# A hybrid layer on one core: the states' single steps split into three parts, VectorE ahead of ScalarE on the scan's bank, the gate's tail on GpSimd and ScalarE

## The chip, the core and the metric

The kernel runs on one core of one Trainium2 chip. A core has a matrix engine (TensorE, PE in the profile; its weight loads are PEld), a vector engine (VectorE, DVE), an activation engine (ScalarE, ACT), a general engine (GpSimd, POOL) and a queue engine that issues DMAs (SyncE, SP). Each engine works through its own queue in order; semaphores tie the queues together. The metric is the time of one execution on the device in microseconds, the median of the runs.

## The reference

One layer of a hybrid decoder is computed for a prompt of 1024 tokens and, with the same weights, for one new token of each of 8 running sequences (1032 columns in all), in 32-bit floats. After a norm, one input projection feeds two mixers: a gated linear recurrence of 8 heads (HGRN2) and a Mamba-2 mixer of 16 heads in two groups. Their outputs go through one output projection, and a gated MLP with a short convolution follows. What matters here is the Mamba-2 mixer:

```python
xbc = silu(causal_dwconv(xbc_r, buf_s, conv_w, conv_b))      # 12 tiles of 128 channels
xs, Bm, Cm = split(xbc)                                      # x: 16 heads of 64; B, C: 2 groups of 128
dt = softplus(dt_r + dt_bias);  A = -exp(a_log)
y, S = ssd_scan(xs * dt, A * dt, Bm, Cm, S0)                 # chunks of 128 tokens
y = y + d * xs
y = rmsnorm(y * silu(z)) * ssm_norm_w                        # the gate, per group of 512 channels
```

For the 8 running sequences the scan has length one: `S = exp(A*dt) * S0 + (xs*dt) outer B` and `y = S . C + d * xs`. All states S are outputs.

## The kernel before

The activations lie transposed, 128 channels on the partitions and the 1032 columns along the free dimension. A 32-bit product is made of three matmuls on split operands (high by high, low by high, high by low). The input projection is a list of jobs, one for each tile of 128 output channels; `in_job` runs one as three chunks of 344 columns with 24 matmuls each, so 72 a job, and after each chunk an `evict` takes the result out of its PSUM bank. The Mamba jobs are x8, x10 (B and C of group 0, made first), x0 to x3 (x of group 0), then x9, x11 (B and C of group 1) and x4 to x7 (x of group 1). After them come z0 to z3 (the gate of group 0), the four jobs of head 0 (f, q, v, sg), z4 to z7 and the rest of the heads. `xbc_evict` and `xbc_close` do the convolution: a copy on ACT, small copies on DVE (L346, L348), one scaling on ACT (L332), three multiply-adds on DVE (L334) and the silu on ACT (L356).

The work between the projections' matmuls comes in streams. `ssd(g)` is the scan of group g: for each of 8 chunks of 128 tokens a front (`ssd_front`) and a back (`ssd_back`). The front loads two blocks csb of cumulated decays, makes exponentials of them on ACT (L530, L531), puts a transpose of B and the product of B and C side by side into one bank `bg`, takes the first out with an ACT copy (L537) and the second, times a triangular mask, with DVE (L538), both into one tile `bt`, transposes x into the bank `xp`, and makes xdt (DVE, L543), xde (POOL, L544) and csb times the masked product (DVE, L546). The back makes the outputs and the next state (yo, st, yd on PE; L563, L569, L579, L582 on DVE; L568 on POOL).

`decode_bc(g)` transposes B and C of the 8 single tokens and writes them to a DRAM scratch bc_d, from which `ssm_decode(g, i)` reads them back, spread over all partitions. `ssm_decode` is the single step of one tile of group g. For each of two halves of the batch it issues three loads (Bb and Cb from bc_d, the state Sd), scales the state on ACT (L627, four instructions), makes Bb times x (DVE, L628), adds it to the state (DVE, L629), stores the state, multiplies it by Cb on POOL (L631) and sums that on DVE (L632). A last small DVE instruction (L633) puts the result back into the tile. All of this is emitted in one go.

The gate's jobs `z` evict through a silu on ACT (L659), multiply on DVE (L660), square on ACT and add up in gacc on POOL or DVE (L665). 36 matmuls (50 for group 1) after a chunk of the fourth, `rstd` makes the norm's factor (L637 to L640), and after the last chunk `tail` multiplies the four tiles of the group by the norm's weight and by gacc, on DVE (L683), and stores them to mix_d. Head 0's levels follow on group 1's tail: `scale` makes products on DVE (L853, L854) and copies on ACT (L856, L857), which PE's matmuls `a` read.

The order on PE is the order in which the program is written: `drive` emits the matmuls of a stream among those of the jobs by a weight, and `after(n, work)` puts work in after n more matmul steps. The other engines' instructions are ordered by a planner which knows dependencies and estimated times; each engine's queue is in order. Loads made through `fetch` are held behind the last weight load.

Of the kernel before, what the change touches and what calls it, by code (L numbers as in the profile page):

```python
# [16 lines left out]
P = 128  # L17
# [33 lines left out]
def hybrid_layer(  # L51
# [19 lines left out]
    def nm(s):  # L71
        cnt[0] += 1
        return f"{s}_{cnt[0]}"
# [18 lines left out]
    def mm(out, lhsT, rhs, start=True, stop=True):  # L92
        PE.matmul(out, lhsT, rhs, start=start, stop=stop)  # L93
# [256 lines left out]
    def xbc_close(j, ext):  # L350
# [6 lines left out]
        A.activation(acc[:, T:NT], acc[:, T + 3:T + 32:4], AF.Silu)  # L357
        return acc

    def xbc_job(j, put):  # L360
        ext = []
        def begin():
            ext.append(xbc_open())
            if j in (5, 7):
                ssm_decode(0, (5, 7).index(j))

        in_job(f"x{j}", OFF_X + j * P, lambda c, cs, ps: xbc_evict(j, ext[0], c, cs, ps), begin=begin, end=lambda: put(xbc_close(j, ext[0])))

# [150 lines left out]
    def ssd_front(g, c, parts):  # L519
        tsl = slice(c * P, (c + 1) * P)  # L520
        hc = c * 16 + g * 8
        lm = []
        for q in range(2):
            csb = half("csb")
            csb3 = csb.rearrange("p (h l) -> p h l", l=P)
            h0 = hc + q * 4
            fetch(csb, cs_d[0, h0:h0 + 4, :].rearrange("h l -> (h l)").unsqueeze(0).to_broadcast([P, 512]))

            for h in range(4):
                A.activation(csb3[:, h, :], csb3[:, h, :], AF.Relu, scale=-1.0, bias=cst[:, h0 + h:h0 + h + 1])  # L530
            A.activation(csb, csb, AF.Exp, scale=-1.0)  # L531
            lm.append(csb3)
        bg = bank("bg")
        PE.transpose(bg[:, 0:P], BT[g][:, tsl], ident)
        mm(bg[:, P:2 * P], BT[g][:, tsl], CT[g][:, tsl])
        bt = small.tile([P, 2, P], F32, tag="bt", bufs=2, name=nm("bt"))
        A.copy(bt[:, 0, :], bg[:, 0:P])  # L537
        V.tensor_tensor(bt[:, 1, :], bg[:, P:2 * P], tri, op=ALU.mult)  # L538
        xp = bank("xp")
        for i in range(4):  # L540
            PE.transpose(xp[:, i * P:(i + 1) * P], Xg[g][i][:, tsl], ident)
        xdt, xde = half("xdt"), half("xde")
        V.tensor_tensor(h64(xdt), h64(xp), b64(dt, hc), op=ALU.mult)  # L543
        G.tensor_tensor(h64(xde), h64(xdt), b64(dec, hc), op=ALU.mult)  # L544
        for csb3 in lm:
            V.tensor_tensor(csb3, csb3, bt[:, 1:2, :].to_broadcast([P, 4, P]), op=ALU.mult)  # L546
        parts[c] = g, c, bt, xdt, xde, lm

    def ssd_back(parts, at_c):
        g, c, bt, xdt, xde, lm = parts.pop(at_c)  # L550
        tsl = slice(c * P, (c + 1) * P)
        hc = c * 16 + g * 8
        Xc = [Xg[g][i][:, tsl] for i in range(4)]
        if c:
            ecs = half("ecs")
            ecs3 = ecs.rearrange("p (j l) -> p j l", l=P)
            for h2 in range(2):
                fetch(ecs3[h2 * 64:(h2 + 1) * 64],
                      cs_d[1, hc:hc + 8, :].rearrange("(j h) l -> h j l", h=2)[h2:h2 + 1].to_broadcast([64, 4, P]))
            yo = bank("yo")  # L560
            for i in range(4):
                mm(yo[:, i * P:(i + 1) * P], S[g][:, i * P:(i + 1) * P], CT[g][:, tsl])
            V.tensor_tensor(ecs, yo, ecs, op=ALU.mult)  # L563
        st = bank("st")
        mm(st, bt[:, 0, :], xde)
        Sn = half("S")
        if c:
            G.tensor_tensor(h64(Sn), h64(S[g]), b64(etot, hc), op=ALU.mult)  # L568
            V.tensor_tensor(Sn, Sn, st, op=ALU.add)  # L569
        else:  # L570
            V.tensor_copy(Sn, st)
        S[g] = Sn
        yd = bank("yd")
        for hh in range(8):
            mm(yd[(hh % 2) * 64:(hh % 2) * 64 + 64, (hh // 2) * P:(hh // 2 + 1) * P],
               xdt[:, hh * 64:(hh + 1) * 64], lm[hh // 4][:, hh % 4, :])
        ya = yd.rearrange("p (j l) -> p j l", l=P)
        if c:
            V.tensor_tensor(ecs, yd, ecs, op=ALU.add)  # L579
            ya = ecs3  # L580
        for i in range(4):
            V.scalar_tensor_tensor(Xc[i], Xc[i], d_bc[:, g * 4 + i:g * 4 + i + 1], ya[:, i, :],  # L582
                                   op0=ALU.mult, op1=ALU.add)
# [16 lines left out]
    def d4(t):  # L600
        return t.rearrange("p (b n) -> p b n", n=P)
# [10 lines left out]
        SP.dma_start(bc_d[2 * g:2 * g + 2].rearrange("i b n -> b i n"), bcr.rearrange("b (i n) -> b i n", n=P))  # L612

    def ssm_decode(g, i):
        j = g * 4 + i
        xdd = small.tile([P, 2, ND], F32, tag="xdd", name=nm("xdd"))
        xdec = Xg[g][i][:, T:NT]
        V.tensor_tensor(xdd[:, 0, :], xdec, ddb[:, 0, j, :], op=ALU.mult)
        for b0 in (0, 4):
            bs = slice(b0, b0 + 4)  # L620
            Bb, Cb = tl("d", "Bb")[:, :512], tl("d", "Cb")[:, :512]
            for t_, r in ((Bb, 2 * g), (Cb, 2 * g + 1)):
                fetch(t_, bc_d[r, bs].rearrange("b n -> (b n)").unsqueeze(0).to_broadcast([P, 512]))
            Sd = tl("ld", "Sd")
            fetch(d4(Sd), state_ssm[0, bs, 2 * j:2 * j + 2].rearrange("b h p n -> (h p) b n"))
            for b in range(4):
                A.activation(d4(Sd)[:, b, :], d4(Sd)[:, b, :], AF.Copy, scale=ddb[:, 1, j, b0 + b:b0 + b + 1])  # L627
            V.tensor_tensor(d4(Bb), d4(Bb), cb(xdd[:, 0, bs]), op=ALU.mult)  # L628
            V.tensor_tensor(Sd, Sd, Bb, op=ALU.add)  # L629
            SP.dma_start(ssm_sample[0, bs, 2 * j:2 * j + 2].rearrange("b h p n -> (h p) b n"), d4(Sd))  # L630
            G.tensor_tensor(Cb, Sd, Cb, op=ALU.mult)  # L631
            V.tensor_reduce(xdd[:, 1, bs], d4(Cb), axis=mybir.AxisListType.X, op=ALU.add)  # L632
        V.scalar_tensor_tensor(xdec, xdec, d_bc[:, j:j + 1], xdd[:, 1, :], op0=ALU.mult, op1=ALU.add)  # L633

    def rstd_of(dst, tmp, ps, n):

# [5 lines left out]
    def ssm_gate(g):  # L642
        acc = []

        def z_job(i):
            j = g * 4 + i

            def begin():
                if i == 0:
                    acc.append(tl("g", "gacc"))  # L650
                if g:
                    ssm_decode(1, i)
                elif i < 2:
                    ssm_decode(0, i + 2)

            def evict(c, cs, ps):
                Y = Xg[g][i][:, cs]
                sz = tl("z", "sz")[:, :CH]
                A.activation(sz, ps, AF.Silu)  # L659
                V.tensor_tensor(Y, Y, sz, op=ALU.mult)  # L660
                if i == 0:
                    A.activation(acc[0][:, cs], Y, AF.Square)
                else:
                    A.activation(sz, Y, AF.Square)
                    (V if g or i == 3 else G).tensor_tensor(acc[0][:, cs], acc[0][:, cs], sz, op=ALU.add)  # L665
                if i == 3:
                    after(36 + 14 * g, lambda: rstd(c))
            in_job(f"z{j}", OFF_Z + j * P, evict, begin=begin)

        def rstd(c):  # L670
            cs = chunks[c]
            ps = bank("ms", "nx")
            mm(ps[:, :CH], ones, acc[0][:, cs])
            rstd_of(acc[0][:, cs], tl("z", "nt")[:, :CH], ps[:, :CH], 512)

            if c == NCH - 1:
                tail()

        def tail():
            for i in range(4):  # L680
                j = g * 4 + i
                Y = Xg[g][i][:, :NT]
                V.scalar_tensor_tensor(Y, Y, col("sn", j), acc[0][:, :NT], op0=ALU.mult, op1=ALU.mult)  # L683
                SP.dma_start(mix_d[8 + j], Y)

        for i in range(4):
            z_job(i)
# [13 lines left out]

    def ssd(g):
        parts = {}
        decode_bc(g)
        yield 6.5
        ssd_front(g, 0, parts)
        for c in range(1, NC):
            yield 2.5
            ssd_front(g, c, parts)
            yield 2.5  # L710
            ssd_back(parts, c - 1)
        yield 3.0
        ssd_back(parts, NC - 1)
        yield 1.0
        ssm_state_out(g)
# [366 lines left out]
                out_job(r0, m, (hf,), r0 == 4)  # L1082

    with tc.manual_schedule(engines={mybir.EngineType.PE}):
        finish("x3")
        drive(ssd(0), 45.5, "x7")
        drive(ssd(1), 45.5, "v0")
        finish("z7")
        for h in range(H):
            drive(head(h, heads[h]), 32.0 if h else 35.0, f"sg{h + 1}" if h < H - 1 else "o12.2")  # L1090
        finish("o12.6")
        for r0 in (0, 4):
            mixes[r0] = mix_load(r0)
# [363 lines left out]
```

## Time and profile before

| | us |
|---|---|
| median of 3 runs | 1786.03 (1785.04 to 1788.24) |
| profiled execution's own time | 1782.61 |
| its span | 1780.9 |
| PE busy | 1725.4 |
| DVE busy | 1119.3 |
| ACT busy | 817.5 |
| POOL busy | 405.3 |

The profiled execution is 3.4 us below the median of the runs shown. The instructions that the change touches lie between about 97 us (job x3) and 420 us (the first levels of head 0): the scan of group 0 from 116 us, its gate's tail at 294 us, the scan of group 1 from about 225 us and its gate's tail at 403 us. In the windows the first column is the stretch, then its length, the busy time of PE, PEld, DVE, ACT and POOL with their instructions, PE's granted clock as a share of full speed, the DMA engines' busy share and GB/s. A line of waits reads: the waiting engine, tile and line, the one it waited for, the sum in us, how often, and the longest. A timeline line reads: start, length, engine, line, operation, out<-in, shapes, and in brackets the idle time just before and what ended it. In groups by tile the three durations are the least, median and greatest in ns, then the first and last start.

### The profile page before, as it was taken

What the parts mean: (1) busy time and instruction counts of PE and PEld (TensorE: products, weight loads), DVE (VectorE), ACT (ScalarE), POOL (GpSimd) and SP (SyncE); (2) the same over time, 40 slices, a digit from 0 to 9 for tenths busy, and PEclk for the clock granted to TensorE, in tenths of its full rate; (3) what the DMA queues carried; (4) which work ended last, traced back from release to release, by engine and by line L of the source; (5) the groups of instructions that cost most, each with busy time, mean ns of one, the idle gap of its engine ahead of it and who ended that gap; (6) DMA issues with size and microseconds to landing.
All of it is one profiled execution on the core that took longest, in us unless ns stands there. A gap on an engine that the chain in (4) does not pass through costs nothing. (4 is left out here: it accounts for less than half of the span.)

```text
span 1780.9 us, 38506 instructions
## 1 busy us (share of the span) xinstructions
PE 1725.4 (97%) x16143; PEld 1675.6 (94%) x16143; DVE 1119.3 (63%) x2011; ACT 817.5 (46%) x1464; POOL 405.3 (23%) x415
## 2 busy tenths in 40 slices
PE   7999899999999999999999978999999999999998
PEld 6998799999999999999899978999999999999997
DVE  6667966575564565458645768666666666445545
ACT  7677688455554454545333435334333344111114
POOL 2113331220110111011000364554445542000001
PEclk9999999999999999999999998999999999999999
DMA  4144634642221222234334432222222225422212
GB/s 154 39 126 126 189 106 132 184 137 98 87 66 51 86 73 78 58 109 155 101 108 133 135 90 72 72 72 78 82 91 72 72 84 203 152 81 90 97 61 96
DMA packets 218019, 182.34 MB, mean 102 GB/s; under 512 B 13388, under 2 KB 195158, under 8 KB 217830
## 3 DMA queue, kind: packets, MB, share of 16 engines
q1 hardware_dynamic: 217558, 179.80, 32.3%
q8 instruction: 126, 2.06, 0.5%
q14 instruction: 47, 0.39, 0.1%
q0 software_dynamic: 288, 0.10, 0.0%
HBM read 141.53 MB, written 38.52 MB: 101 GB/s over the span
## 5 line engine op out<-in xcount | busy, mean ns | idle before, releaser
L93 PE MATMUL mm<-hh,wh 128*128 128x344 f32 x1248 | 405.3, 325 | 0.3 <-issue 0.2
L93 PE MATMUL mm<-hl,wh 128*128 128x344 f32 x1248 | 404.5, 324 | 0.0
L93 PE MATMUL mm<-hh,wl 128*128 128x344 f32 x1248 | 402.0, 322 | 0.0
L93 PEld LDWEIGHTS mm<-hh,wh 128*128 128x128 f32 x1248 | 235.0, 189 | 3.9 <-issue 2.6
L93 PEld LDWEIGHTS mm<-hl,wh 128*128 128x128 f32 x1248 | 235.2, 189 | 2.4 <-issue 0.9
L93 PEld LDWEIGHTS mm<-hh,wl 128*128 128x128 f32 x1248 | 235.3, 189 | 2.2 <-issue 1.5
L183 ACT CAST wh<-ws 128x1024 fp32r<-128x1024 f32 x96 | 100.5, 1047 | 242.8 <-PE dn L93 135.3
L93 PE MATMUL ub<-ul,wh 128*128 128x258 f32 x704 | 200.4, 285 | 4.3 <-DVE ul L1144 4.3
L93 PE MATMUL ub<-uh,wh 128*128 128x258 f32 x704 | 200.3, 285 | 2.0 <-ACT uh L1143 2.0
L93 PE MATMUL ub<-uh,wl 128*128 128x258 f32 x704 | 200.2, 284 | 0.0
L93 PE MATMUL dn<-ah,wh 128*128 128x256 f32 (+1 forms) x640 | 181.1, 283 | 1.2 <-DVE x L1387 1.2
L93 PE MATMUL dn<-al,wh 128*128 128x256 f32 (+1 forms) x640 | 180.6, 282 | 0.0
L93 PE MATMUL dn<-ah,wl 128*128 128x256 f32 (+1 forms) x640 | 180.2, 282 | 0.0
L184 DVE TENSOR_TENSOR wl<-ws,wh 128x1024 fp32r<-128x1024 f32 x96 | 126.4, 1317 | 72.4 <-ACT wh L183 71.4
L93 PE MATMUL mm<-mh,wh 128*128 128x258 f32 x512 | 147.7, 288 | 11.2 <-DVE x L1040 8.3
L93 PE MATMUL ua<-ul,wh 128*128 128x258 f32 x528 | 149.4, 283 | 0.9 <-DVE ul L1144 0.9
L93 PE MATMUL ua<-uh,wh 128*128 128x258 f32 x528 | 149.2, 283 | 0.0
L93 PE MATMUL ua<-uh,wl 128*128 128x258 f32 x528 | 148.4, 281 | 0.0
L93 PE MATMUL mm<-ml,wh 128*128 128x258 f32 x512 | 145.8, 285 | 0.7 <-DVE ml L999 0.7
L93 PE MATMUL mm<-mh,wl 128*128 128x258 f32 x512 | 145.9, 285 | 0.0
L93 PEld LDWEIGHTS ub<-ul,wh 128*128 128x128 f32 x704 | 134.5, 191 | 5.0 <-DVE ul L1144 5.0
L93 PEld LDWEIGHTS ub<-uh,wh 128*128 128x128 f32 x704 | 134.0, 190 | 2.5 <-ACT uh L1143 2.5
(347 smaller groups left out, 3942.8 us busy)
## 6 DMA issues: line engine op xcount, KB each, us to landing
ws<-in_w_in_dram SPq DMA_DIRECT2D x52, 512.0 KB
ws<-in_w_up_dram SPq DMA_DIRECT2D x44, 512.0 KB
ws<-in_w_out_dram SPq DMA_DIRECT2D x24, 512.0 KB
act_d<-val SPq DMA_DIRECT2D x22, 516.0 KB
al<-act_d SPq DMA_DIRECT2D x22, 516.0 KB
ws<-in_w_down_dram SPq DMA_DIRECT2D x22, 512.0 KB
ml<-mix_d SPq DMA_DIRECT2D x48, 172.0 KB
csb<-cs_d SPq DMA_DIRECT2D x32, 256.0 KB
```

What stands on the lines that cost most here:

```text
L93: PE.matmul(out, lhsT, rhs, start=start, stop=stop)
L183: A.copy(wh[:, :n], ws[:, :n])
L184: V.tensor_tensor(wl[:, :n], ws[:, :n], wh[:, :n].bitcast(F32), op=ALU.subtract)
```

## The change

- `ssm_decode` is cut into three: the loads when it is called, the states (scaling, product, sum, store, POOL product) 30 matmul steps later, the outputs (the two sums over Cb and the last small instruction) 30 steps after that. The small xdd product moves from the call to the states.
- The single steps of group 0 begin with the jobs x3, x11, x5 and x7 in place of x5, x7, z0 and z1. Those of group 1 stay at z4 to z7.
- `decode_bc(0)` is emitted after job x2, ahead of x3, in place of after x3.
- In `ssd_front` the tile bt is parted into bt and bc; DVE's masked product out of the bank bg is written ahead of ACT's copy out of the same bank.
- In the gate's tail the DVE instruction on 128x1032 is replaced by a POOL multiply by gacc and an ACT scaling by the norm's weight, in place, four of each per group.

```diff
--- before.py
+++ after.py
@@ -357,12 +357,15 @@
         A.activation(acc[:, T:NT], acc[:, T + 3:T + 32:4], AF.Silu)
         return acc
 
+
+    DEC0 = (3, 11, 5, 7)
+
     def xbc_job(j, put):
         ext = []
         def begin():
             ext.append(xbc_open())
-            if j in (5, 7):
-                ssm_decode(0, (5, 7).index(j))
+            if j in DEC0:
+                ssm_decode(0, DEC0.index(j))
 
         in_job(f"x{j}", OFF_X + j * P, lambda c, cs, ps: xbc_evict(j, ext[0], c, cs, ps), begin=begin, end=lambda: put(xbc_close(j, ext[0])))
 
@@ -533,9 +536,9 @@
         bg = bank("bg")
         PE.transpose(bg[:, 0:P], BT[g][:, tsl], ident)
         mm(bg[:, P:2 * P], BT[g][:, tsl], CT[g][:, tsl])
-        bt = small.tile([P, 2, P], F32, tag="bt", bufs=2, name=nm("bt"))
-        A.copy(bt[:, 0, :], bg[:, 0:P])
-        V.tensor_tensor(bt[:, 1, :], bg[:, P:2 * P], tri, op=ALU.mult)
+        bt, bc = (small.tile([P, P], F32, tag=s_, bufs=2, name=nm(s_)) for s_ in ("bt", "bc"))
+        V.tensor_tensor(bc, bg[:, P:2 * P], tri, op=ALU.mult)
+        A.copy(bt, bg[:, 0:P])
         xp = bank("xp")
         for i in range(4):
             PE.transpose(xp[:, i * P:(i + 1) * P], Xg[g][i][:, tsl], ident)
@@ -543,7 +546,7 @@
         V.tensor_tensor(h64(xdt), h64(xp), b64(dt, hc), op=ALU.mult)
         G.tensor_tensor(h64(xde), h64(xdt), b64(dec, hc), op=ALU.mult)
         for csb3 in lm:
-            V.tensor_tensor(csb3, csb3, bt[:, 1:2, :].to_broadcast([P, 4, P]), op=ALU.mult)
+            V.tensor_tensor(csb3, csb3, bc.unsqueeze(1).to_broadcast([P, 4, P]), op=ALU.mult)
         parts[c] = g, c, bt, xdt, xde, lm
 
     def ssd_back(parts, at_c):
@@ -562,7 +565,7 @@
                 mm(yo[:, i * P:(i + 1) * P], S[g][:, i * P:(i + 1) * P], CT[g][:, tsl])
             V.tensor_tensor(ecs, yo, ecs, op=ALU.mult)
         st = bank("st")
-        mm(st, bt[:, 0, :], xde)
+        mm(st, bt, xde)
         Sn = half("S")
         if c:
             G.tensor_tensor(h64(Sn), h64(S[g]), b64(etot, hc), op=ALU.mult)
@@ -612,10 +615,11 @@
         SP.dma_start(bc_d[2 * g:2 * g + 2].rearrange("i b n -> b i n"), bcr.rearrange("b (i n) -> b i n", n=P))
 
     def ssm_decode(g, i):
+
         j = g * 4 + i
         xdd = small.tile([P, 2, ND], F32, tag="xdd", name=nm("xdd"))
         xdec = Xg[g][i][:, T:NT]
-        V.tensor_tensor(xdd[:, 0, :], xdec, ddb[:, 0, j, :], op=ALU.mult)
+        ts_ = []
         for b0 in (0, 4):
             bs = slice(b0, b0 + 4)
             Bb, Cb = tl("d", "Bb")[:, :512], tl("d", "Cb")[:, :512]
@@ -623,14 +627,26 @@
                 fetch(t_, bc_d[r, bs].rearrange("b n -> (b n)").unsqueeze(0).to_broadcast([P, 512]))
             Sd = tl("ld", "Sd")
             fetch(d4(Sd), state_ssm[0, bs, 2 * j:2 * j + 2].rearrange("b h p n -> (h p) b n"))
-            for b in range(4):
-                A.activation(d4(Sd)[:, b, :], d4(Sd)[:, b, :], AF.Copy, scale=ddb[:, 1, j, b0 + b:b0 + b + 1])
-            V.tensor_tensor(d4(Bb), d4(Bb), cb(xdd[:, 0, bs]), op=ALU.mult)
-            V.tensor_tensor(Sd, Sd, Bb, op=ALU.add)
-            SP.dma_start(ssm_sample[0, bs, 2 * j:2 * j + 2].rearrange("b h p n -> (h p) b n"), d4(Sd))
-            G.tensor_tensor(Cb, Sd, Cb, op=ALU.mult)
-            V.tensor_reduce(xdd[:, 1, bs], d4(Cb), axis=mybir.AxisListType.X, op=ALU.add)
-        V.scalar_tensor_tensor(xdec, xdec, d_bc[:, j:j + 1], xdd[:, 1, :], op0=ALU.mult, op1=ALU.add)
+            ts_.append((bs, Bb, Cb, Sd))
+
+        def states():
+            V.tensor_tensor(xdd[:, 0, :], xdec, ddb[:, 0, j, :], op=ALU.mult)
+            for bs, Bb, Cb, Sd in ts_:
+                for b in range(4):
+                    A.activation(d4(Sd)[:, b, :], d4(Sd)[:, b, :], AF.Copy,
+                                 scale=ddb[:, 1, j, bs.start + b:bs.start + b + 1])
+                V.tensor_tensor(d4(Bb), d4(Bb), cb(xdd[:, 0, bs]), op=ALU.mult)
+                V.tensor_tensor(Sd, Sd, Bb, op=ALU.add)
+                SP.dma_start(ssm_sample[0, bs, 2 * j:2 * j + 2].rearrange("b h p n -> (h p) b n"), d4(Sd))
+                G.tensor_tensor(Cb, Sd, Cb, op=ALU.mult)
+            after(30, outputs)
+
+        def outputs():
+            for bs, Bb, Cb, Sd in ts_:
+                V.tensor_reduce(xdd[:, 1, bs], d4(Cb), axis=mybir.AxisListType.X, op=ALU.add)
+            V.scalar_tensor_tensor(xdec, xdec, d_bc[:, j:j + 1], xdd[:, 1, :], op0=ALU.mult, op1=ALU.add)
+
+        after(30, states)
 
     def rstd_of(dst, tmp, ps, n):
 
@@ -650,8 +666,6 @@
                     acc.append(tl("g", "gacc"))
                 if g:
                     ssm_decode(1, i)
-                elif i < 2:
-                    ssm_decode(0, i + 2)
 
             def evict(c, cs, ps):
                 Y = Xg[g][i][:, cs]
@@ -680,7 +694,8 @@
             for i in range(4):
                 j = g * 4 + i
                 Y = Xg[g][i][:, :NT]
-                V.scalar_tensor_tensor(Y, Y, col("sn", j), acc[0][:, :NT], op0=ALU.mult, op1=ALU.mult)
+                G.tensor_tensor(Y, Y, acc[0][:, :NT], op=ALU.mult)
+                A.activation(Y, Y, AF.Copy, scale=col("sn", j))
                 SP.dma_start(mix_d[8 + j], Y)
 
         for i in range(4):
@@ -701,7 +716,8 @@
 
     def ssd(g):
         parts = {}
-        decode_bc(g)
+        if g:
+            decode_bc(g)
         yield 6.5
         ssd_front(g, 0, parts)
         for c in range(1, NC):
@@ -1082,6 +1098,8 @@
                 out_job(r0, m, (hf,), r0 == 4)
 
     with tc.manual_schedule(engines={mybir.EngineType.PE}):
+        finish("x2")
+        decode_bc(0)
         finish("x3")
         drive(ssd(0), 45.5, "x7")
         drive(ssd(1), 45.5, "v0")
```

## The prediction

> **What bounds the kernel now.** I read the page's busy table first, then PE's waits in the stretch the change touches, then the engines' load in 20 us windows.
>
> ```profile
> PE 1725.4 (97%) x16143; PEld 1675.6 (94%) x16143; DVE 1119.3 (63%) x2011; ACT 817.5 (46%) x1464; POOL 405.3 (23%) x415
> ```
>
> TensorE (PE) works 1725.4 of 1780.9 us. A change on other engines can only give or take the 55 us in which PE stands still, and what a lowered clock adds. So each step below is priced by what it does to a wait of PE. These are PE's waits between 110 and 420 us:
>
> ```profile
> PE xp L541 <- DVE ecs L563: 3.0, 2, 2.2
> PE yo L93 <- DVE S L569: 2.6, 1, 2.6
> PE a L93 <- DVE q L854: 2.5, 1, 2.5
> PE xp L541 <- ACT xbc L356: 1.2, 1, 1.2
> PE yd L93 <- DVE xdt L543: 0.8, 1, 0.8
> ```
>
> All but the third lie in the scan of group 0; together they are 3.0 + 2.6 + 1.2 + 0.8 = 7.6 us. The windows say why (columns: length, then PE, PEld, DVE, ACT, POOL busy, clock, DMA):
>
> ```profile
> 180.00:200.00 20.00, 18.23 (x130) 15.80 (x129) 18.69 (x32) 15.82 (x37) 7.63 (x8) 1.00 0.67 201
> 200.00:220.00 20.00, 16.72 (x105) 14.76 (x104) 19.22 (x33) 9.82 (x24) 5.17 (x4) 0.91 0.62 168
> ```
>
> ```profile
> 280.00:300.00 20.00, 20.00 (x139) 18.83 (x138) 16.55 (x31) 19.84 (x37) 2.25 (x2) 1.00 0.43 140
> ```
>
> ```profile
> 206.10:209.50 3.40, 3.06 (x10) 2.21 (x10) 3.40 (x6) 1.28 (x4) 2.35 (x2) 0.50 0.19 52
> 410.90:414.30 3.40, 3.04 (x132) 2.93 (x133) 2.78 (x6) 1.14 (x3) 0.00 (x0) 0.50 0.56 159
> ```
>
> VectorE (DVE) is full from 180 to 220 us, where steps 2 and 3 of group 0 meet the convolutions. Right after each of the two waits of over 2.5 us the clock stands at half for 3.4 us, which costs 1.7 us of work apiece. ScalarE (ACT) is full at 280 to 300, though PE does not wait there.
>
> **Part 1: the step in three parts, 30 matmuls apart, and the new order of the scan's bank.** DVE's waits from 95 to 420 us, and the place where one reaches PE:
>
> ```profile
> DVE bt L538 <- ACT bt L537: 23.3, 10, 4.9
> DVE xdd L632 <- POOL Cb L631: 15.0, 11, 3.2
> DVE Bb L628 <- DMA Bb<-bc_d: 13.7, 8, 3.0
> ```
>
> ```profile
> 147.76 3.23 POOL L544 TENSOR_TENSOR xde<-xdt,dec 128x512 f32<-128x512 f32 x1 [1.08 <-DVE xdt L543]
> ```
>
> ```profile
> 148.80 1.29 DVE L629 TENSOR_TENSOR Sd<-Sd,Bb 128x512 f32<-128x512 f32 x2
> ```
>
> DVE ends the two state additions at 150.1 and then its queue holds the reduction (L632), which needs POOL's product Cb; POOL is in xde until 150.99. Behind the reduction stand ecs (L563) and with it PE's 2.2 us. With outputs 30 matmuls later (139 pass in the 20 us of the last full window, so 30 take 4.3 us) the products are done when the reduction comes up. bc first on DVE takes away its 23.3 us of waiting on ACT's copy; ACT then waits for DVE instead, and behind it stand csb's exponentials and the evictions, which have slack outside 280 to 300. Moving steps 2 and 3 from z0 and z1 to x5 and x7 takes 2 x 4.1 us of DVE work (per step two each of Bb, Sd and the reduction, rows below) out of the full stretch 180 to 220. I take the 7.6 us and one slow clock stretch of 1.7 as gone, and leave 0.6 for a short remainder: **-8.7 us**. Bounds: -9.3, and -4.5 if the waits behind DVE go only by half.
>
> **Part 2: step 0 now at x3, step 1 at x11, and decode_bc(0) ahead of x3.** Per step: six loads and two stores on SP, eight ACT scales, eight large and small DVE operations, two POOL products. The first front of the scan needs x3 itself:
>
> ```profile
> L627 ACT ACTIVATE Sd<-Sd,ddb x64: 384/393/410, 128.3 to 370.7; 128x128 f32<-128x128 f32 x64
> ```
>
> ```profile
> L628 DVE TENSOR_TENSOR Bb<-Bb,xdd x16: 675/692/1532, 126.0 to 365.7; 128x512 f32<-128x512 f32 x16
> L629 DVE TENSOR_TENSOR Sd<-Sd,Bb x16: 680/686/1161, 148.8 to 371.2; 128x512 f32<-128x512 f32 x16
> ```
>
> ```profile
> L632 DVE TENSOR_REDUCE xdd<-Cb x16: 672/686/687, 153.3 to 373.5; 128x4 f32<-128x512 f32 x16
> ```
>
> ```profile
> 121.29 0.53 SPq L175 DMA_DIRECT2D Bb<-bc_d  x1
> 121.87 0.42 SPq L175 DMA_DIRECT2D Cb<-bc_d  x1
> 122.34 0.43 SPq L175 DMA_DIRECT2D Sd<-in_state_ssm_dram  x1
> ```
>
> On DVE, x2's and x3's eviction copies and x3's convolution:
>
> ```profile
> 97.26 0.17 DVE L346 COPY ext<-mm 128x8 f32<-128x8 f32 x1
> ```
>
> ```profile
> 108.32 0.17 DVE L346 COPY ext<-mm 128x8 f32<-128x8 f32 x1 [1.45 <-ACT ext L344]
> ```
>
> ```profile
> 110.44 4.03 DVE L334 SCALAR_TENSOR_TENSOR xbc<-ext,vcol,xbc 128x1056 f32<-128x1056 f32 x3
> ```
>
> Then x3's silu on ACT and the first front on PE:
>
> ```profile
> 114.51 1.06 ACT L356 ACTIVATE xbc<-xbc 128x1024 f32<-128x1024 f32 x1 [0.52 <-DVE xbc L334]
> ```
>
> ```profile
> 116.21 0.60 PE L541 MATMUL xp<-ident,xbc 128*128 128x128 f32 x4
> ```
>
> x3's silu ends at 115.6 and PE's transposes that read it begin at 116.2: 0.6 us of slack. In the changed instruction order DVE has both halves of step 0 and the first Bb of step 1 ahead of x3's last eviction copies. A load takes 4.7 us from issue to use (121.29 to 126.0) for Bb, 6.0 for Sd (122.34 to 128.3). x2's last eviction stands at 97.3, so bcr follows there and the write of bc_d can be issued at about 98; I let it land at 101, since csb's loads were issued just ahead of it. Bb is then there at 104.5, half 0 ends its Sd at 107.3 (Bb 0.7, one convolution pass 1.3, Sd 0.7), POOL's product and the reduction bring 109.3, half 1's Sd, product and reduction 112.0, step 1's Bb 113. x3's copies then stand at 113 instead of 108.3, and the convolution (4.0, with another Bb between) ends at 119 instead of 114.5. On ACT the Sd scale of step 1 stands ahead of the silu and waits for a load that is issued only after step 0's Sd is stored, at about 110.5: there at 116.5. Two table loads, an exponential, scales and a copy later the silu ends at 120.5 to 122. PE has come to it at 116.4: **+5.0 us**, and +1.7 for the slow clock that follows a wait this long. Bounds 0 (loads and stores land 4 us sooner than in those rows) and 7.
>
> **Part 3: the gate's tail.** Four DVE operations of 1.29 us go; four POOL multiplies and four ACT scalings of the same 128x1032 come, in a chain. No POOL operation of that size is in the trace:
>
> ```profile
> L665 POOL TENSOR_TENSOR gacc<-gacc,sz x6: 909/926/1427, 236.9 to 262.0; 128x344 f32<-128x344 f32 x6
> ```
>
> ```profile
> L631 POOL TENSOR_TENSOR Cb<-Sd,Cb x16: 1261/1294/2159, 152.0 to 372.0; 128x512 f32<-128x512 f32 x16
> ```
>
> ```profile
> L1151 POOL TENSOR_TENSOR sm<-sm,x x4: 1205/1588/1638, 1017.3 to 1072.2; 128x516 f32<-128x516 f32 x4
> ```
>
> The medians of the first two give (1294 - 926)/168 = 2.19 ns an element, so 1294 + 520 x 2.19 = 2.43 us; their minima give 2.35; twice the third gives 3.2. I take d = 2.5, near the two rows with the steadier times. The GPSIMD Engine Reference of the Trainium skill (section 3.1) has about 2.6 cycles per element at 1.2 GHz for a two-input operation; by that estimate d is 2.24 and each tail 1.0 us shorter. The rows here carry the sum.
>
> Group 0's tail begins at 294. ACT's queue now holds the four scalings, each waiting for its POOL product, ahead of head 0's f, csb's exponentials, the copy bt and q's evictions:
>
> ```profile
> 294.27 4.90 DVE L683 SCALAR_TENSOR_TENSOR xbc<-xbc,vcol,gacc 128x1032 f32<-128x1032 f32 x4
> ```
>
> ```profile
> 295.14 1.24 ACT L792 ACTIVATE f<-f,lbt 128x1032 f32<-128x1032 f32 x1
> ```
>
> ```profile
> 299.97 0.24 ACT L537 COPY bt<-bg 128x128 f32<-128x128 f32 x1
> ```
>
> ```profile
> 302.06 0.46 ACT L799 ACTIVATE q<-mm 128x344 f32<-128x344 f32 x1
> ```
>
> ```profile
> 308.62 0.27 PE L534 MATMUL bg<-ident,xbc 128*128 128x128 f32 x1
> ```
>
> The last scaling ends at 294.1 + 4d + 1.25 = 305.4. f (1.25), three csb rows, a table load, an exponential and three more rows follow, so bt is copied at about 300.75 + 4d = 310.8 and q's bank is free at 303.1 + 4d = 313.1. PE wants bt's bank at 308.6 and, after the transposes of that front, q's bank at about 309.4: **+3.8 us** in all, and half a chance of the slow clock, +0.9. At d = 2.35 and 3.2 the wait is 3.2 and 6.6.
>
> Group 1's tail begins at 403.1, while head 0 is in its levels:
>
> ```profile
> 410.42 0.62 ACT L856 COPY k<-f 128x512 f32<-128x512 f32 x1 [1.45 <-DVE f L853]
> 411.03 0.62 ACT L857 COPY v<-q 128x512 f32<-128x512 f32 x1
> ```
>
> ```profile
> 412.34 0.73 PE L93 MATMUL a<-v,k 128*16 128x16 f32 x64
> ```
>
> Those two copies feed that matmul and stand behind the scalings: 403 + 4d + 1.25 + 1.25 = 415.5 against 412.34, **+3.2 us** net (the old 2.5 us wait and its slow clock are in both). Bounds 2.6 and 6.0.
>
> **Sum.** -8.7 + 5.0 + 1.7 + 3.8 + 0.9 + 3.2 = +5.9 against the profiled execution's 1782.61 us, which is 3.4 below the median of the runs shown; with that distance kept, 1786.0 + 5.9, about 1792. Since the front's wait rests on landing times and is bounded by 0 below and 7 above, I round toward the lower side: 1791.
>
> **The rivals.** *The first front is on time.* If the loads of step 0 land some 4 us sooner, x3's silu ends by 116.4 and part 2 costs nothing. For it: bc_d is 8 KB and the weight load is not in front of it. Against: a 4.7 us row for the same load. Time: 1786.0 - 8.7 + 3.8 + 0.9 + 3.2 = 1785.2, with d = 2.35 some 1784: no change. *The tails leave the path.* DVE no longer holds its 4.9 us of tail at 403, and head 0's L853 and L854, on which PE's 2.5 us wait at 411 hangs, stood behind that tail. If PE's copies are not held by ACT in its place, that wait and its slow clock go too: 1786.0 - 8.7 + 6.7 - 2.5 - 1.7 = 1779.8, the faster side. It decides from 403 + 4d + 2.5 below 409.8, so d below 1.1, or from the scalings coming later in ACT's order than I read. Against it: no row of POOL at that size is near; for it: ACT stood idle for 1.45 us ahead of its copy at 410.4.
>
> ```profile
> L544 POOL TENSOR_TENSOR xde<-xdt,dec x16: 1037/1044/3228, 117.7 to 311.0; 128x512 f32<-128x512 f32 x16
> ```
>
> *POOL slowed by DVE.* xde took 3.2 us at 147.76 against a median of 1.04, while DVE ran two-input work. If the four products of a tail are stretched like that by 0.6 us each, both tails grow by 2.4: 1796. The GPSIMD Engine Reference of the Trainium skill (section 1) says the memory interfaces are shared with VectorE and contended by its two-input operations; the 3.2 us row agrees, and it speaks against the change. *The gain does not come*, because ACT waiting for DVE at bt is late as often as DVE was: half of part 1, 1796.
>
> **How the numbers follow.** Forecast 0.42; front on time 0.23; tails off the path 0.20; POOL slowed or the gain missing 0.15. What a measurement here can tell from no change is 0.2%, 3.6 us. The forecast is slower but for a twentieth, the second is mostly no change, the third faster, the last slower; the second's near bound adds 0.07 to faster: faster 0.27, same 0.20, slower 0.53. The range 1779 to 1799 runs from the third case to beyond the last and leaves out what lies further.
>
> **What would show it.** Right: PE's waits on ecs (L563 of before), S and xdt gone; one new PE wait of 3 to 7 us near 116 on xbc's silu with the clock at 0.5 behind it; one near 309 on bt or the q bank's eviction; PE's matmuls a from v and k some 3 us later after group 1's tail; POOL rows of 128x1032 at 2.35 to 3.2 us. Wrong: x3's silu ending before 117, PE without a wait at 309, or POOL products under 2 us.

## The result and the profile after

The changed kernel takes 1797.62 us (median of 6, 1795.15 to 1801.49) against 1785.16 us (median of 6, 1782.04 to 1788.24): a ratio of 1.0073, 95% interval 1.0056 to 1.009, or 12.5 us slower. The forecast was slower, 1791, with 1779 to 1799 as its range; it had started from 1786.03, the median of the three runs shown then. The profiled execution after took 1797.12 us, its span is 1794.8.

PE's waits between 110 and 430 us in the changed kernel (same columns as before):

```profile
PE a L93 <- DVE q L870: 6.5, 1, 6.5
PE xp L544 <- ACT xbc L356: 4.1, 1, 4.1
PE xp L544 <- DVE ecs L566: 2.1, 2, 1.7
PE bg L537 <- ACT bt L541: 1.9, 1, 1.9
PE ms L93 <- DVE vd L839: 1.6, 1, 1.6
PE mm L93 <- ACT sz L673: 1.4, 1, 1.4
PE mm L93 <- ACT q L815: 1.3, 1, 1.3
PE ms L93 <- DVE nt L654: 0.9, 1, 0.9
PE yo L93 <- DVE S L572: 0.6, 1, 0.6
PE a L93 <- ACT v L873: 0.5, 1, 0.5
PE sT L597 <- DVE S L572: 0.3, 1, 0.3
```

The scan's waits (ecs, yo, sT here) shrank from 8.2 us, the 7.6 of the prediction and 0.6 on sT, to 3.0. Three places are new: x3's silu (4.1), the front behind group 0's tail (1.9 and 1.3), and PE's first large wait in head 0, which was 2.5 us and is 6.5. The stretches of slow clock (a granted clock of half) are these, in windows laid on them:

```profile
120.20:123.60 3.40, 3.04 (x11) 3.04 (x12) 2.62 (x4) 2.03 (x8) 1.76 (x2) 0.52 0.08 25
311.30:314.70 3.40, 3.40 (x12) 3.40 (x13) 3.26 (x9) 1.59 (x6) 0.00 (x0) 0.52 0.58 154
420.90:427.70 6.80, 5.30 (x141) 5.16 (x142) 5.27 (x9) 5.83 (x10) 0.31 (x1) 0.51 0.61 245
```

They are 13.6 us long in place of 6.8, so another 3.4 us of work is lost. PE's waits of over 0.25 us in the stretch sum to 21.2 us against 12.0 before. 9.2 + 3.4 = 12.6 us is the loss that the traces place; the two profiled executions differ by 14.5, and the other 1.9 us are not placed.

**The front at x3.** DVE's rows of the changed kernel:

```profile
109.77 0.69 DVE L646 TENSOR_REDUCE xdd<-Cb 128x4 f32<-128x512 f32 x1 [1.47 <-POOL Cb L641]
...
111.24 0.17 DVE L346 COPY ext<-mm 128x8 f32<-128x8 f32 x1
...
116.10 2.67 DVE L334 SCALAR_TENSOR_TENSOR xbc<-ext,vcol,xbc 128x1056 f32<-128x1056 f32 x2
```

and ACT's:

```profile
119.45 1.06 ACT L356 ACTIVATE xbc<-xbc 128x1024 f32<-128x1024 f32 x1
```

x3's copies stand at 111.2 in place of 108.3, behind two reductions that wait for POOL. The convolution ends at 118.8 and the silu at 120.5.

**The tail.** POOL's group of products:

```profile
L697 POOL TENSOR_TENSOR xbc<-xbc,gacc x8: 2432/2655/3376, 292.1 to 418.4; 128x1032 f32<-128x1032 f32 x8
```

A POOL product takes 2.43 us at least and 2.66 in the median. Beside group 1's four products (one row of POOL), DVE looks like this:

```profile
409.88 11.33 POOL L697 TENSOR_TENSOR xbc<-xbc,gacc 128x1032 f32<-128x1032 f32 x4 [6.01 <-DVE gacc L656]
```

```profile
410.05 2.80 DVE L869 TENSOR_TENSOR f<-f,tt 128x512 f32<-128x512 f32 x1
412.78 3.44 DVE L184 TENSOR_TENSOR wl<-ws,wh 128x1024 fp32r<-128x1024 f32 x1
416.14 2.85 DVE L809 TENSOR_SCALAR k<-f 128x1032 f32<-128x1032 f32 x1
418.91 2.85 DVE L870 TENSOR_TENSOR q<-q,tt 128x512 f32<-128x512 f32 x1
421.68 0.68 DVE L869 TENSOR_TENSOR k<-f,tt 128x512 f32<-128x512 f32 x1
```

This had not been in the forecast. Before, the same four instructions (k is L793 there, f and q are L853 and L854) came right behind the tail:

```profile
407.96 0.69 DVE L793 TENSOR_SCALAR k<-f 128x1032 f32<-128x1032 f32 x1
408.57 1.22 DVE L184 TENSOR_TENSOR wl<-ws,wh 128x1024 fp32r<-128x1024 f32 x1
409.70 0.69 DVE L853 TENSOR_TENSOR f<-f,tt 128x512 f32<-128x512 f32 x1
410.31 0.69 DVE L854 TENSOR_TENSOR q<-q,tt 128x512 f32<-128x512 f32 x1
```

Now they take 11.9 us, one for each POOL product, and the first after POOL's last product is back at 0.68. Read one by one, each of the four ends 0.5 to 1.1 us after the POOL product that was at work when it began, so about its own length later. POOL waits as well: the four products take 2.43, 2.89, 3.34 and 2.81 us. PE's wait of 6.5 us ends with the fourth DVE instruction.

### The profile page after: what moved, and what is told of

Its sections match the earlier page's. It is cut to its first block, busy times and chain, and to the rows that moved or that the text cites. A ratio compares the mean times of both kernels' runs of the same rounds, so it can differ in the third digit from the quotient of the medians.

```text
span 1794.8 us, 38517 instructions
## 1 busy us (share of the span) xinstructions
PE 1728.4 (96%) x16143; PEld 1679.2 (94%) x16143; DVE 1122.0 (63%) x2003; ACT 826.6 (46%) x1472; POOL 432.4 (24%) x423
## 5 line engine op out<-in xcount | busy, mean ns | idle before, releaser
L184 DVE TENSOR_TENSOR wl<-ws,wh 128x1024 fp32r<-128x1024 f32 x96 | 131.3, 1368 | 71.7 <-ACT wh L183 70.9
```

Of the source, the lines that this page charges most:

```text
L184: V.tensor_tensor(wl[:, :n], ws[:, :n], wh[:, :n].bitcast(F32), op=ALU.subtract)
```

## The experiments

Ratios are to runs of the kernel before on the same chip, with 95% intervals; a thousandth is 1.8 us. Times in the expectations start from the 1785.2 us of the kernel before, so a ratio is held against them on that.

**The tail alone, and the change without it.** First `tail_back`, the change with the tail as before:

```diff
-                G.tensor_tensor(Y, Y, acc[0][:, :NT], op=ALU.mult)
-                A.activation(Y, Y, AF.Copy, scale=col("sn", j))
+                V.scalar_tensor_tensor(Y, Y, col("sn", j), acc[0][:, :NT], op0=ALU.mult, op1=ALU.mult)
```

> The changed kernel with the gate's tail back as one DVE instruction per tile; the rest of the change stays. If the two tails cost what the trace shows (waits of 3.2 us and a slow clock of 1.7 us at group 0; 7.0 us and two slow windows in place of 2.5 us and one at group 1, so 4.9 + 6.2 = 11.1 us), this comes to 1797.6 - 11.1 = 1786.5 us. If the tails are a smaller part and the moved steps cost more downstream, it stays at 1790 or above.

Measured: 0.9985 (0.9972 to 0.9998), so 1782.5 on 1785.2 and 4 us below what was expected. The next, `tail_only`, is the kernel before with the tail of the change:

> The kernel before with only the gate's tail as POOL multiply and ACT scaling. If the tail is a cost of its own, 1785.2 + 9 to 11 = 1794 to 1796 us, with PE waits near 309 and 411 us. If the tail costs only because the moved steps made ACT and DVE late, 1787 or less.

Measured: 1.0075 (1.006 to 1.009), 1798.6 and some 3 us above the expected range. There are waits of 1.3 and 1.4 us near 310 and of 3.1 at 331, and PE's wait in head 0 comes again:

```profile
PE a L93 <- DVE q L855: 6.5, 1, 6.5
```

The tail is a loss of its own: 13 us by itself, and 15.7 us beside the rest of the change (1.0073 against 0.9985). The rest of the change is a gain of some 2.7 us.

**What in the tail costs.** The forecast's step was ACT's queue behind the scalings; the trace pointed to POOL holding DVE up. `tail_vec_mul` takes POOL out and leaves the chain to ACT:

```diff
-                G.tensor_tensor(Y, Y, acc[0][:, :NT], op=ALU.mult)
+                V.tensor_tensor(Y, Y, acc[0][:, :NT], op=ALU.mult)
```

> The changed kernel with the tail's multiply on DVE in place of POOL, the ACT scaling behind it as in the change. ACT still waits for each multiply, for 1.3 us each in place of 2.5. If the loss is POOL holding up DVE's instructions (wl 3.4 in place of 1.2 us, k 2.9 in place of 0.7), all DVE rows return to their lengths and the time is within 1 us of the kernel with the tail back, 1786 to 1788 us. If the loss is the ACT queue waiting behind the products whatever engine makes them, half of it stays: 1790 to 1792.

Measured: 0.9984 (0.997 to 0.9998), the same as with the tail back; on 1785.2 that is 1782.3, below the times expected, as with `tail_back`. Its DVE rows have their old lengths. This takes both the hold and the long products away, so `tail_scale_first` takes ACT's wait alone away, by the order of the two:

```diff
-                G.tensor_tensor(Y, Y, acc[0][:, :NT], op=ALU.mult)
                 A.activation(Y, Y, AF.Copy, scale=col("sn", j))
+                G.tensor_tensor(Y, Y, acc[0][:, :NT], op=ALU.mult)
```

> The changed kernel with the tail's ACT scaling ahead of the POOL multiply (for this the scaling needs only the gated tile), so that ACT waits for no POOL product; POOL does the same four multiplies. If the cost is ACT's queue waiting behind the scalings (the step of the prediction), the time falls to that of the kernel with the tail back, about 1786.5 us. If the cost at group 1 is POOL holding DVE's instructions up, PE's wait on DVE of about 6 us near 420 stays with its slow clock: 1791 to 1794 us.

Measured: 1.0049 (1.0032 to 1.0066), 1793.9, at the upper end of what POOL holding DVE up was to give. The waits at bt and q's bank near 309 are gone, but one of 3.4 us comes at 331, PE's wait in head 0 is 7.2 us, and ACT itself waits there for DVE. The waits of PE, ACT's row, and POOL's and DVE's rows in group 0's tail:

```profile
PE a L93 <- DVE q L870: 7.2, 1, 7.2
PE xp L544 <- ACT xbc L356: 3.9, 1, 3.9
PE sT L597 <- DVE S L572: 3.4, 1, 3.4
```

```profile
423.95 0.62 ACT L873 COPY v<-q 128x512 f32<-128x512 f32 x1 [8.26 <-DVE q L870]
```

```profile
293.03 10.65 POOL L698 TENSOR_TENSOR xbc<-xbc,gacc 128x1032 f32<-128x1032 f32 x4 [6.55 <-DVE gacc L656]
```

```profile
292.87 5.21 DVE L585 SCALAR_TENSOR_TENSOR xbc<-xbc,d_bc,ecs 128x128 f32<-128x128 f32 x3
298.01 3.43 DVE L184 TENSOR_TENSOR wl<-ws,wh 128x1024 fp32r<-128x1024 f32 x1
301.37 0.28 DVE L540 TENSOR_TENSOR bc<-bg,tri 128x128 f32<-128x128 f32 x1
301.57 0.68 DVE L546 TENSOR_TENSOR xdt<-xp,dt 128x512 f32<-128x512 f32 x1
```

The three instructions on 128x128 took 0.35 us each before. The first still does, ahead of POOL's first product; the other two take 2.5 us each. The two that read a PSUM bank (bg, xp) keep their lengths, although POOL works until 303.7. `tail_pool_thirds` leaves ACT's wait and shortens the hold:

```diff
-                G.tensor_tensor(Y, Y, acc[0][:, :NT], op=ALU.mult)
+                for cs in chunks:
+                    G.tensor_tensor(Y[:, cs], Y[:, cs], acc[0][:, cs], op=ALU.mult)
```

> The changed kernel with each POOL multiply of the tail cut into three of 344 columns, some 0.95 us each. If a POOL instruction keeps DVE's two-input instructions out until it ends, each of DVE's four instructions ahead of PE's wait near 422 us now waits for a third: lengths of 1 to 2 us in place of 2.8 to 3.4, PE's wait of 6.5 us falls to 1 to 3 us, and the time to 1790 to 1793 us. If the two only share the memory's rate while both work, the rows of DVE stay at about 2.8 us in sum and the time stays at 1797 us.

Measured: 1.0042 (1.0027 to 1.0057), 1792.7, the far end of what the hold would give. DVE's rows are as it says:

```profile
405.96 1.08 DVE L870 TENSOR_TENSOR f<-f,tt 128x512 f32<-128x512 f32 x1
406.96 1.96 DVE L184 TENSOR_TENSOR wl<-ws,wh 128x1024 fp32r<-128x1024 f32 x1
408.84 1.42 DVE L871 TENSOR_TENSOR q<-q,tt 128x512 f32<-128x512 f32 x1
```

PE's wait on DVE has gone, not shrunk to 1 to 3 us, but now the other path ends last. PE's wait, and ACT's rows behind it:

```profile
PE a L93 <- ACT v L874: 7.0, 1, 7.0
```

```profile
411.07 1.16 ACT L699 ACTIVATE xbc<-xbc,vcol 128x1032 f32<-128x1032 f32 x1 [4.94 <-POOL xbc L698]
...
413.72 2.20 ACT L699 ACTIVATE xbc<-xbc,vcol 128x1032 f32<-128x1032 f32 x2 [0.18 <-POOL xbc L698]
415.83 1.23 ACT L809 ACTIVATE f<-f,lbt 128x1032 f32<-128x1032 f32 x1
416.97 0.60 ACT L873 COPY k<-f 128x512 f32<-128x512 f32 x1
417.48 0.61 ACT L874 COPY v<-q 128x512 f32<-128x512 f32 x1
```

That is the step as forecast: the copies stand behind four scalings, each behind its product. If two paths of like length lead to this wait, easing both must shorten it where easing either did not. `thirds_scale_first` has the scaling first and the thirds:

> The changed kernel with both causes of the tail eased at once: the ACT scaling ahead of the multiplies, and each POOL multiply cut into three of 344 columns. If POOL holding DVE up and ACT's queue behind the scalings are two paths to the same wait of PE, each hidden by the other, PE's wait of 6.5 to 7.2 us near 420 us falls to 1 to 3 us here and the time to 1786 to 1790 us (ratio 0.999 to 1.002). If POOL's work itself, in whatever pieces, is what PE waits for, it stays near the kernel with thirds alone: 1.004.

Measured: 1.0007 (0.9998 to 1.0017), 1786.4, and PE's wait in head 0 is that of the kernel before:

```profile
PE a L93 <- DVE q L871: 2.6, 2, 2.5
```

So both readings held, and at this wait each was hidden by the other: it stayed at 7 us with either eased, and fell to 2.5 with both. In time the two are not hidden so. On 1785.2, against the 1.0073 of the change, the scaling first brought 4.3 us, the thirds 5.5, and both 11.8; where the single gains come from was not placed. Some 4 us of the tail's 15.7 are left (1.0007 against 0.9985); DVE's rows beside the thirds are still 1.3 to 2.0 us long there, and what that costs was not measured.

**The parts in the scan.** `split_only` is the kernel before with `ssm_decode` as in the change, called at its old places:

> The kernel before with the step in three parts alone, at its old places x5, x7, z0 and z1. If DVE's wait for POOL's product is what PE's 2.2 us at 156 us hangs on, that wait goes and the others (0.9, 0.8, 2.6 with its slow clock, 0.6, 1.2), where DVE is full, stay: a ratio of 0.9985 to 0.999. If the split spreads the full stretch as well, all go: 0.995.

Measured: 1.0007 (0.9996 to 1.0018), no change. The wait of DVE that it was to take away is no less, 15.5 us after 15.0:

```profile
DVE xdd L643 <- POOL Cb L638: 15.5, 10, 3.2
```

PE's wait at 156 is 1.4 us in place of 2.2, and others came. Only PE's instructions are in the written order; on the planned engines the 30 steps did not keep DVE from standing at the sum before the product is there. `bank_only` has the bank's order alone:

```diff
-        A.copy(bt[:, 0, :], bg[:, 0:P])
-        V.tensor_tensor(bt[:, 1, :], bg[:, P:2 * P], tri, op=ALU.mult)
+        V.tensor_tensor(bc, bg[:, P:2 * P], tri, op=ALU.mult)
+        A.copy(bt, bg[:, 0:P])
```

> The kernel before with DVE ahead of ScalarE on the scan's bank alone. DVE's 23 us of waiting for bt goes; if that idle time was on no path to PE, no change (ratio 0.9995 to 1.0005). If it is what fills DVE between 180 and 220 us, PE's waits there (0.9 + 0.8 + 2.6 + 0.6 and 1.7 of slow clock) shrink: 0.997 to 0.998. If ACT waiting for DVE holds evictions, 1.001 or more.

Measured: 0.9982 (0.997 to 0.9994). PE's wait at 156 goes to 0.2 us and those on xdt and yo (0.8 and 2.6) below 0.3. Those on ecs (3.4 in all) and sT (2.0) are longer than before, and a slow clock comes at 193 in place of 206: of the scan's 8.2 us, 5.8 are left. DVE's wait on bt's copy turns into one on csb's exponentials, of like size, and its wait for POOL's products stays:

```profile
DVE csb L546 <- ACT csb L531: 19.8, 14, 3.6
DVE xdd L632 <- POOL Cb L631: 17.6, 11, 3.2
```

What DVE gets done ahead of this wait that it did not ahead of the other stays open. `bank_split` is both:

> The kernel before with DVE ahead of ScalarE on the bank and the step in three parts, at its old places; tail and decode_bc as before. If the split is worth nothing by itself (its products are waited for as before), the ratio is that of the bank order alone, 0.998. If it only pays where DVE is no longer held up at the bank, 0.995 to 0.9965.

Measured: 0.9988 (0.9974 to 1.0002). The split adds nothing to the bank's order. Nor, in time, do the moved steps: `tail_back`, which differs from this in their places and decode_bc's alone, had 0.9985. In the traces the move does show: the scan's waits are 7.4 us with a slow clock in `bank_split`, and some 3.5 without one in `tail_back`, which has 3.1 us at x3's front in their place. `later_steps` tried to take the new wait at x3 out of that:

```diff
-    DEC0 = (3, 11, 5, 7)
+    DEC0 = (11, 4, 5, 7)
```

> The kernel with the tail back as one DVE instruction per tile, and the four steps of group 0 at the jobs x11, x4, x5 and x7 in place of x3, x11, x5 and x7. If PE's wait for x3's silu near 120 us comes from step 0 standing ahead of x3's convolution, it goes (3.1 to 4.4 us, and the slow clock where it comes): 3 to 6 us below the kernel with the tail back, so a ratio of 0.995 to 0.997 to the kernel before. If the steps only move the wait to another front, the ratio stays at 0.998 to 0.999.

Measured: 1.001 (1.0 to 1.0021), a miss. The wait at x3 is 1.5 us in place of 3.1, but xdt is late at other fronts:

```profile
PE yd L93 <- DVE xdt L546: 5.0, 4, 2.3
```

**A version faster than both.** PE's wait of 2.5 us at 411 us hangs on the 4.9 us block of DVE's tail. `bank_tail_spread16` is `bank_only` with the block opened:

```diff
+            def tile_(i):
                 j = g * 4 + i
...
             for i in range(4):
+                after(1 + 16 * i, lambda i=i: tile_(i))
```

> The kernel before with DVE ahead of ScalarE on the bank, and the four DVE instructions of the gate's tail 16 matmul steps apart in place of one after the other. If PE's wait of 2.5 to 2.7 us at 411 us with its slow clock of 1.7 us hangs on the 4.9 us block of the tail, half of that block now stands behind head 0's products and the wait goes: 0.9955 to 0.9965. If head 1's tiles, which come free behind the tail's stores, are then late, 0.998 or more.

Measured: 0.9952 (0.9939 to 0.9964), 8.6 us below the kernel before. Two of the four now stand behind head 0's products on DVE, and PE's wait is 0.5 us:

```profile
400.74 2.49 DVE L683 SCALAR_TENSOR_TENSOR xbc<-xbc,vcol,gacc 128x1032 f32<-128x1032 f32 x2
...
405.48 0.69 DVE L856 TENSOR_TENSOR q<-q,tt 128x512 f32<-128x512 f32 x1
...
407.62 2.50 DVE L683 SCALAR_TENSOR_TENSOR xbc<-xbc,vcol,gacc 128x1032 f32<-128x1032 f32 x2
```

`steps_tail_spread16` adds the moved steps in three parts:

> All of the change but the tail (the steps in three parts and earlier, decode_bc ahead of x3, DVE first on the bank), with the four DVE instructions of the gate's tail 16 matmul steps apart. If the moved steps are worth nothing beside the bank order (their gain in the scan is paid again in the wait for x3's silu), the ratio is within 0.001 of the same kernel without them, 0.994 to 0.996. If the steps carry a gain of their own that the tail's block hid, 0.993 or less; if a loss, 0.997.

Measured: 0.9968 (0.9957 to 0.998), between what no worth and a loss were to give. It overlaps with the one before, and tells no gain of the steps.

## Why the prediction was right, and where it was off

- **Part 1, -8.7 us.** In the trace of after the old waits of the scan come to 3.0 in place of 7.6 + 0.6 us, and the slow clock at 206 is gone: -6.9. The wait on ecs, which was to be gone, stays with 2.1 of its 3.0 us. One reading was off: the 1.2 us on xbc's silu stand at 226 us, at the first front of group 1's scan and not in group 0's. And the cause was in part put in the wrong place. Of the sentence "with outputs 30 matmuls later the products are done when the reduction comes up" nothing is left: DVE still waits 20.0 us for the products in the change and 15.5 with the split alone, which by itself is no gain. PE's 2.2 us at 156, which the prediction hung on this, went with the bank's order alone. Moving steps 2 and 3 does take waits out of the scan (`bank_split` against `tail_back`), but x3's front costs 3.1 us there, and by time the two are alike. The bank's order alone gives 0.9982, and nothing was found to add to it but the opened tail.
- **Part 2, +6.7 us.** Right in place, way and nearly in size: a wait of 4.1 us on x3's silu and 1.7 us of slow clock, 5.8. The silu ended at 120.5, the near end of the forecast 120.5 to 122; the loads came some 1 to 2 us sooner than taken. Parts 1 and 2 together were forecast at -2.0, and the change without its tail measured -2.7 (0.9985).
- **Part 3, the POOL product.** 2.5 us was taken, with 2.35 and 3.2 as bounds; 2.43, 2.66 and 3.38 were measured (least, median, most). The straight line through the two shorter shapes had given 2.43, the least measured.
- **Part 3, group 0, +4.7.** 1.9 + 1.3 us of wait on just the two things named, bt's bank and q's eviction, and the slow clock of 1.7: 4.9. Both waits are gone in `tail_scale_first`, so they were ACT's queue behind the products, as forecast. That the slow clock came was half a chance.
- **Part 3, group 1, +3.2.** This is the term that failed: 6.5 + 0.5 us of wait and 3.4 us of slow clock, less the old 2.5 and 1.7, is +6.2. "Those two copies feed that matmul and stand behind the scalings" was a true path, as `tail_pool_thirds` shows, but not the one that ended last. The forecast costed the POOL product on POOL's and ACT's queues and took DVE as freed of 4.9 us. The rival *POOL slowed by DVE* had the pair right and the direction half: POOL's products were 9% longer in the median, and DVE's instructions three to seven times as long. Its 1796 lies near the measured time by luck, since it took each product as 0.6 us longer, and nothing for DVE.
- **Not forecast.** 1.4 us on sz and 1.1 more on ms while group 1's gate runs. They do not need the tail: `tail_back` has 1.2 and 1.0, `bank_only` 1.0 and 1.2. Nor do they need the bank's order: `split_only`, without it, has 1.3 and 1.4. What brings them stays open.

The terms as read from the trace are -6.9 + 5.8 + 4.9 + 6.2 + 2.5 = 12.5 us; as forecast they were 5.9, taken down to 5. The slower side was told and the time lies in the range, 1.4 us below its upper end, but the loss was forecast at less than half: 3.0 us of the difference are group 1's tail, 2.5 the waits on sz and ms, 1.8 part 1.

That these terms come to just the difference of the medians is in part chance, since the two profiled executions differ by 14.5 us; and their split is less sure than their sum. By the runs without and with the tail (0.9985, 1.0073) the tails are worth 15.7 us and the rest -2.7, where the terms of the trace have 11.1 and +1.4. In the trace without the tail the front's wait is 3.1 us and has no slow clock, 2.7 us less than with it; the 1.9 us that the trace did not place may be of the tail too. This stays open.

## What to carry to other kernels

Work given to POOL did not run beside DVE's work where both read two operands from SBUF. Before moving an instruction off DVE, look what DVE does at that time, and count each such instruction as waiting for the POOL instruction in progress. When taking one of two suspected causes away leaves a wait as it was, take both away before calling either innocent; here PE's wait in head 0 fell only with both. And a delay written in steps of the one engine whose order is written by hand need not move the engines whose order is planned: see whether the wait is gone in the trace after, as it was not here (15.5 us after 15.0).

## What the runs showed of the hardware

DVE instructions with two SBUF operands, and the 128x1032 TENSOR_SCALAR with one (2.85 us after 0.69), made no headway beside POOL's TENSOR_TENSOR, although their rows overlap: in the changed kernel one got through for each product of 2.4 to 3.4 us, and with products cut into thirds they took 1.1 to 2.0 us. POOL waited in turn: in group 1's tail, behind such an instruction, a product took 2.8 to 3.3 us in place of 2.43, and the xde of 3.23 us in the kernel before (1.04 in the median) ended 0.9 us after the last of four such instructions on DVE. DVE instructions that read one operand from PSUM kept their 0.28 and 0.68 us meanwhile. The GPSIMD Engine Reference of the Trainium skill (section 1) names this contention for two SBUF inputs and for two-port modes; the rows of two SBUF inputs agree. That the TENSOR_SCALAR runs in a two-port mode no row shows. The lengths show a wait for the whole instruction of the other engine rather than a lower rate.

The clock of PE fell to half after a wait of 2.1 us at 191 us in `bank_tail_spread16`, and after 2.7 us at 411 us in `bank_only`, but not after 3.1 us at 121 us nor 2.7 us at 410 us in `tail_back`; after waits of 4.4 us (`tail_vec_mul`) and 6.5 us (the changed kernel) it stayed low for 6.8 us in place of 3.4. TensorE: Matmul & The Clock Gate of the Trainium skill (What's actually happening) says that the window over which activity is judged runs freely, 3.4 us long. That fits stretches of 3.4 and 6.8 us. It would also let like waits end differently by luck, though no run shows where a window begins. That a whole idle window is needed, as the same section of the Trainium skill says, does not fit: 2.1 us sufficed.
